# A scan's products one level behind and tied to projections, its states in two steps, and modulation passes in groups of four

## The chip, the cores and the metric

The kernel runs on one core of a Trainium2 chip. The metric is the device time of one execution in microseconds (us); of several executions the median is quoted. An execution profiled by the hardware shows each engine's instructions: TensorE (PE, with its weight loads as PEld), VectorE (DVE), ScalarE (ACT), GpSimd (POOL), and the DMA queue of SyncE (SP).

## What is computed

The reference is one inference step of a small diffusion backbone with two layers, width 1024, for 128 context tokens and 512 latent tokens, all in 32-bit floats. Layer 0 mixes its 640 tokens by neighbourhood attention and by bidirectional gated linear attention (four heads, key width 64, value width 128); layer 1 by grouped-query attention. Each layer ends in a ConvFFN, and each sublayer is modulated by vectors that come from the conditioning through a matrix of 1024 x 6144 a layer. The change concerns the linear attention:

```python
def step(s, inp):                       # one chunk of 64 tokens, one direction
    qc, kc, vc, gc = inp
    bcum = jnp.cumsum(gc.astype(jnp.float32), axis=2)
    o_inter = jnp.einsum('bhid,bhde->bhie', qc * jnp.exp(bcum).astype(qc.dtype), s)
    ...
    att = jnp.einsum('bhid,bhjd,bhijd->bhij', qc, kc, decay)
    o = o_inter + jnp.einsum('bhij,bhje->bhie', att, vc)
    k_dec = kc * jnp.exp(blast - bcum).astype(kc.dtype)
    s_new = exp(blast) * s + jnp.einsum('bhjd,bhje->bhde', k_dec, vc)
```

and the modulation, `jax.nn.silu(cvec) @ w + bias`.

## The kernel before

Every large matrix product is a projection of three matmuls per tile, since operands are split into a high and a low part. `step` (L149 to L153) makes tiles named mm with 320 columns, `tokens_major` (L592 to L594) makes tiles named tm with 256 columns. Their weights come as ws tiles by DMA (L127); ScalarE rounds them to wh (L111), and VectorE or GpSimd forms the rest wl (L112).

The linear attention works on two head pairs, 0 and 1, in pieces that `layer0` calls in the order of `ORDER = ("a0", "s0", "a1", "o0", "q0", "s1", "o1")`: a for `gla_scores`, s for `gla_states`, o for `gla_out`; q puts the neighbourhood's query and key projection at the head of the queue.

- `gla_scores` takes seven levels (the products of tile lev) and then two wide ones, 32 and 64 (tile off). A level is a chain over four engines: VectorE subtracts cumulated gates into ea (L852) and eb (L853), ScalarE takes exponentials (L832), GpSimd multiplies ea by keys (L858) and VectorE multiplies eb by queries (L859); then 40 small matmuls on TensorE (L872), which use both, a masked copy acc on VectorE (L877) and an addition on GpSimd (L879). The wide levels' matmuls (L894, L898) are copied by ScalarE into att (L903), and VectorE sets the levels' sums in (L907).
- `gla_states` makes, for each direction, decayed keys kd on ScalarE and GpSimd, four transposes kdt on TensorE (L933), a copy kt on ScalarE (L935), eight matmuls ds (L940) and, on VectorE, state updates S (L945, L946).
- `gla_out` makes decayed queries qd and the outputs go (L965 to L968).

Between the steps of these pieces the kernel hands out other work by `fill.some(n, m)`: n steps of a queue of projections and m modulation passes from a list aside. A pass is the DMA of a 128 x 512 tile wa (L313, three buffers) and two multiply-and-sum instructions on VectorE over it (L316, outputs junk and wa). 48 passes lie in this stage. `fill.some(0, 99)` before s0 hands out all that are left.

The code's order isn't the final one: a list scheduler sets each engine's stream, in which queue work given out by `fill.some` has priority. Each engine then executes its stream in order. Behind the scan stand the neighbourhood's loads on SP: values vw (L782), their context vc (L784) and the bias tiles (L1064), which the attention's scores nas add (L1075) before they are transposed (napt, L1083).

## Time and profile before

| | us |
|---|---|
| median of 3 runs (1725.24 to 1729.24) | 1727.22 |
| profiled execution | 1725.67 |
| its span, first to last instruction | 1723.9 |

The profiled execution has 1.77 us outside its span. Its mean granted TensorE clock is 0.975 of full speed. The profile is read in this order: the busy shares, the span cut into stretches, what TensorE waited for in the scan's stretch, and the timeline around those waits. A length in the timeline is that of one instruction or of a run of like ones; matmuls overlap, so their pitch is the difference of two starts.

### The profile page before, as it was taken

How to read it: one execution, taken by the hardware profiler on the slowest of the kernel's cores; microseconds unless marked ns; L12 is line 12 of the kernel's file. 1: busy time of each engine (PE TensorE's matmuls, PEld its weight loads, DVE VectorE, ACT ScalarE, POOL GpSimd, SP SyncE). 2: the span in 40 equal slices, each digit the busy share in tenths (PEclk: the TensorE clock that was granted, in tenths of full speed). 3: DMA queues.
4: the chain of work that ended last, by engine and by line, in shares of the span. 5: the costliest groups of instructions: out<-in, count | busy, mean ns of one | idle time of the engine just before them, and what ended most of it. 6: DMA issues, size and time to landing. Idle time of an engine off the chain costs nothing.

```text
span 1723.9 us, 33442 instructions
## 1 busy us (share of the span) xinstructions
PE 1633.0 (95%) x13142; PEld 1560.4 (91%) x13142; DVE 1255.2 (73%) x2767; ACT 741.9 (43%) x1681; POOL 205.5 (12%) x473
## 2 busy tenths in 40 slices
PE   7969698999999999999999999999999999999997
PEld 6868687879999999999998888888999999999997
DVE  5899944875899989996656987885776544663664
ACT  4443254453533323322335676775453322331342
POOL 2235441310200000000003310100100000000001
PEclk8999899999999999999998999999999999999999
DMA  8623323332254455454232200120222222222222
GB/s 318 210 88 134 102 81 106 91 93 98 84 167 160 147 164 185 153 151 132 70 120 82 76 21 14 43 63 24 76 74 75 73 74 74 75 76 83 73 68 69
DMA packets 68014, 175.22 MB, mean 102 GB/s; under 512 B 7920, under 2 KB 9744, under 8 KB 66832
## 3 DMA queue, kind: packets, MB, share of 16 engines
q1 hardware_dynamic: 67024, 171.48, 30.7%
q8 instruction: 103, 1.69, 0.4%
q0 software_dynamic: 832, 1.60, 0.3%
q14 instruction: 55, 0.45, 0.1%
HBM read 165.71 MB, written 7.34 MB: 100 GB/s over the span
## 4 chain that ended last, share of the span: by engine, by line
PE 78%; DVE 13%; DMA 3%; ACT 2%; issue 2%; SPq 1%; POOL 0%; ACTq 0%; DVEq 0%; POOLq 0%
PE mm L153 66%; PE gpo L1310 2%; DVE wa L316 2%; DVE junk L316 2%; PE gpt L1298 1%; DMA wa<-in_ada_wt_dram 1%; PE gs L1289 1%; DVE wl L112 1%; PE gs L1290 1%; DVE mx L1036 1%; PE napo L1102 1%; PE ss L410 1%; DVE eb L853 1%; DMA bias<-in_na_bias_dram 1%; DVE eb L859 1%
## 5 line engine op out<-in xcount | busy, mean ns | idle before, releaser
L153 PE MATMUL mm<-hh,wl 128*128 128x320 f32 x2080 | 651.0, 315 | 9.2 <-DVE wl L112 4.1
L153 PE MATMUL mm<-hl,wh 128*128 128x320 f32 x2080 | 647.7, 312 | 0.4 <-DVE hl L456 0.4
L153 PE MATMUL mm<-hh,wh 128*128 128x320 f32 x2080 | 641.3, 311 | 0.0
L111 ACT CAST wh<-ws 128x512 fp32r<-128x512 f32 x376 | 228.5, 614 | 435.3 <-PE mm L153 401.9
L153 PEld LDWEIGHTS mm<-hh,wl 128*128 128x128 f32 x2080 | 394.0, 190 | 19.2 <-issue 9.0
L153 PEld LDWEIGHTS mm<-hl,wh 128*128 128x128 f32 x2080 | 395.1, 190 | 2.7 <-DVE h L445 1.2
L153 PEld LDWEIGHTS mm<-hh,wh 128*128 128x128 f32 x2080 | 393.5, 190 | 0.6 <-issue 0.2
L112 DVE TENSOR_TENSOR wl<-ws,wh 128x512 fp32r<-128x512 f32 x348 | 239.1, 689 | 146.5 <-ACT wh L111 145.3
L153 PE MATMUL mm<-glo,wh 128*128 128x320 f32 x704 | 217.7, 310 | 0.0
L153 PE MATMUL mm<-ghi,wh 128*128 128x320 f32 x704 | 217.7, 310 | 0.0
L153 PE MATMUL mm<-ghi,wl 128*128 128x320 f32 x704 | 215.8, 310 | 0.0
L488 DVE SCALAR_TENSOR_TENSOR x<-mm,mod,x 128x192 f32<-128x192 f32 (+2 forms) x240 | 96.9, 435 | 88.9 <-PE mm L153 88.0
L153 PEld LDWEIGHTS mm<-ghi,wl 128*128 128x128 f32 x704 | 132.3, 189 | 1.3 <-issue 1.3
L153 PEld LDWEIGHTS mm<-glo,wh 128*128 128x128 f32 x704 | 133.0, 189 | 0.0
L153 PEld LDWEIGHTS mm<-ghi,wh 128*128 128x128 f32 x704 | 132.8, 189 | 0.1
L316 DVE SCALAR_TENSOR_TENSOR junk<-wa,sb 128x512 f32<-128x512 f32 x160 | 116.9, 734 | 6.7 <-DMA wa<-in_ada_wt_dram 6.4
L316 DVE SCALAR_TENSOR_TENSOR wa<-wa,sb 128x512 f32<-128x512 f32 x160 | 118.2, 745 | 0.3
L522 POOL MEMSET u<- 128x1 f32 x88 | 8.5, 98 | 761.1 <-DVE gate L515 426.6
L525 ACT COPY u<-mm 128x320 f32<-128x320 f32 x88 | 37.7, 431 | 87.8 <-PE mm L153 82.1
L592 PE MATMUL tm<-wl,hh 128*128 128x256 f32 x200 | 58.9, 300 | 7.4 <-ACT v L601 4.4
L1042 ACT ACTIVATE gp<-gs,mx,rq 128x640 f32<-128x640 f32 x64 | 57.0, 891 | 17.3 <-DVE mx L1038 11.6
L528 ACT COPY u<-mm 128x192 f32<-128x192 f32 x88 | 28.4, 323 | 79.8 <-PE mm L153 79.8
(302 smaller groups left out, 2432.5 us busy)
## 6 DMA issues: line engine op xcount, KB each, us to landing
ws<-in_wu_dram SPq DMA_DIRECT2D x88, 512.0 KB, 3.5
wa<-in_ada_wt_dram SPq DMA_DIRECT2D x160, 256.0 KB, 3.1
ws<-in_wd_dram SPq DMA_DIRECT2D x32, 448.0 KB, 3.8
aw<-in_ada_w_dram SPq DMA_DIRECT2D x8, 1024.0 KB, 14.2
ws<-in_w_ab_dram SPq DMA_DIRECT2D x16, 512.0 KB, 10.5
ws<-in_wd_dram SPq DMA_DIRECT2D x16, 512.0 KB, 3.6
x<-in_xT_dram SPq DMA_DIRECT2D x16, 320.0 KB, 4.5
ws<-in_w_gqa_dram SPq DMA_DIRECT2D x10, 512.0 KB, 3.5
```

The costliest lines, as they stand in the source:

```text
L111: nc.scalar.copy(hi, src)
L112: eng.tensor_tensor(lo, src, hi, ALU.subtract)
L153: nc.tensor.matmul(ps, x, y[:, s], start=st, stop=sp_)
L316: nc.vector.scalar_tensor_tensor(w if v else junk, w, 1.0, cs[v, j], ALU.mult, ALU.mult, accum_out=acc[:, k, v, j:j + 1])
L410: nc.tensor.matmul(ps[0:rows, c:c + 2], part[:, t], onesd, start=True, stop=True)
L488: nc.vector.scalar_tensor_tensor(x[:, b:e], ps[:, b - HN * h:e - HN * h], gate[:, v, m:m + 1], old[:, b:e], ALU.mult, ALU.add)
L525: nc.scalar.copy(u[:, 1:321], ps)
L528: nc.scalar.copy(u[:, 321:513], ps[:, 0:192])
L592: nc.tensor.matmul(ps, hh[:, s], wlo, start=(k == 0), stop=False)
L853: nc.vector.tensor_tensor(v(eb), sides(NT, h, 1), sides(g, f, 0), ALU.subtract)
L1042: nc.scalar.activation(dst, src, AF.Exp, bias=mx[:, i:i + 1], accum_out=sm[:, i:i + 1], **kw)
L1310: last = nc.tensor.matmul(po[64 * f:64 * f + 64, 0:128], vs[t][:, 64 * kv:64 * kv + 64], mates[f]["x"][:, 128 * t:128 * t + 128], start=(t ...
```

## The change

Four things are changed in the code. Products of a level (matmuls, masked copy, addition) are made after the next level's sides have been requested, with one more `fill.some(RLEV)` before level 64. Matmuls of products, transposes and states are tied behind the newest projection matmul that the queue has given out, so the scheduler can't put them ahead of it. `gla_states` makes both directions' transposes and copies first and then both directions' matmuls and updates. And passes come four at a time at each s and o piece, with the rest after the last piece.

```diff
@@ -146,11 +146,13 @@
 
         return part
 
+    newest = [None]
+
     def step(ps, w, k, hh, hl, h, start, stop):
         whi, wlo = w(k)
         s = slice(h * HN, h * HN + HN)
         for (x, y, st, sp_) in ((wlo, hh, start, False), (whi, hl, False, False), (whi, hh, False, stop)):
-            nc.tensor.matmul(ps, x, y[:, s], start=st, stop=sp_)
+            newest[0] = nc.tensor.matmul(ps, x, y[:, s], start=st, stop=sp_).ins
 
     def together(srcs, H, done, make=None, raws=None, n=1024):
 
@@ -240,7 +242,14 @@
 
 
         def __init__(self):
-            self.queue, self.aside, self.owed, self.after = [], [], 0.0, None
+            self.queue, self.aside, self.owed, self.after, self.newest = [], [], 0.0, None, None
+
+        def behind(self):
+
+            tie = ExitStack()
+            if self.newest is not None:
+                tie.enter_context(tc.issue_after(self.newest))
+            return tie
 
...
@@ -263,6 +272,7 @@
                     self.queue.pop(0)
                 else:
                     n -= 1
+                    self.newest = newest[0]
 
...
@@ -591,7 +601,7 @@
                     whi, wlo = ws[k // 4](k % 4)
                     nc.tensor.matmul(ps, hh[:, s], wlo, start=(k == 0), stop=False)
                     nc.tensor.matmul(ps, hl[:, s], whi, start=False, stop=False)
-                    nc.tensor.matmul(ps, hh[:, s], whi, start=False, stop=(k == KD - 1))
+                    newest[0] = nc.tensor.matmul(ps, hh[:, s], whi, start=False, stop=(k == KD - 1)).ins
...
@@ -757,15 +767,17 @@
                     att.update(gla_scores(m, kg[m], qg[m], cum[m], fill))
                 elif kind == "s":
                     fill.until(g_vg)
-                    fill.some(0, 99)
+                    fill.some(0, SST)
                     gla_states(m, kg[m], cum[m], vg, S, fill)
                 elif kind == "o":
+                    fill.some(0, SST)
                     last = gla_out(m, qg[m], cum[m], vg, att, S, OT, fill)
                 else:
                     fill.first(nxt)
 
             for p in ORDER:
                 piece(p[0], int(p[1]))
+            fill.some(0, 99)
...
@@ -861,15 +873,15 @@
 
         accs = C("acc")
         acc, tmp = accs[:, 0:320], accs[:, 320:640]
-        for li, h in enumerate(LEVELS):
-            A, B = (k, q) if h == 0 else level(h)
+        def products(li, A, B):
             ps = PS("lev")
...
+            with fill.behind():
+                for t in range(5):
...
@@ -877,27 +889,38 @@
             nc.vector.tensor_tensor(w.rearrange("p (e t i) -> p e t i", e=2, i=32), pv, mk, ALU.mult)
             if li:
                 nc.gpsimd.tensor_tensor(acc[:, 0:320], acc[:, 0:320], tmp[:, 0:320], ALU.add)
+
+
+        ready = None
+        for li, h in enumerate(LEVELS):
+            sides = (li, k, q) if h == 0 else (li, *level(h))
+            if ready:
+                products(*ready)
+            ready = sides
             fill.some(RLEV, SLEV)
         A32, B32 = level(32)
+        products(*ready)
+        fill.some(RLEV)
         A64, B64 = level(64)
         fill.some(ROFF, SOFF)
         big, small = PS("off"), PS("offx")
         res = {}
         blocks = [(e, slice(64 * e, 64 * e + 64), t, big[:, e, 128 * t:128 * t + 128] if t < 4 else small[:, e, 0:128])
                   for e in range(2) for t in range(5)]
-        for width in (32, 64):
...
+        with fill.behind():
+            for width in (32, 64):
...
@@ -926,19 +949,25 @@
             nc.gpsimd.tensor_tensor(x[:, 0:NT], x[:, 0:NT], k[:, 0:NT], ALU.mult)
             expo(de, end)
             kd[d], dec[d] = x, de
-        for d in range(2):
-            tiles = (0, 1, 2, 4) if d == 0 else (3, 2, 1, 4)
+        order = [(0, 1, 2, 4), (3, 2, 1, 4)]
+        kts = []
+        for d, tiles in enumerate(order):
             pt = P1("kdt")
-            for i, t in enumerate(tiles):
-                nc.tensor.transpose(pt[:, 128 * i:128 * i + 128], kd[d][:, 128 * t:128 * t + 128], ident)
+            with fill.behind():
+                for i, t in enumerate(tiles):
+                    nc.tensor.transpose(pt[:, 128 * i:128 * i + 128], kd[d][:, 128 * t:128 * t + 128], ident)
             kt = T("kt", "v2", n=512)
             nc.scalar.copy(kt[:, 0:512], pt)
-            ds = P1("ds")
-            for i, t in enumerate(tiles):
-                for e, pe in col_pairs():
-                    h = 2 * m + e
-                    nc.tensor.matmul(ds[pe, 128 * i:128 * i + 128], kt[:, 128 * i + 64 * e:128 * i + 64 * e + 64],
-                                     vg[t][:, 128 * h:128 * h + 128], start=True, stop=True)
+            kts.append(kt)
+            fill.some(RST / 2)
+        for d, tiles in enumerate(order):
+            kt, ds = kts[d], P1("ds")
+            with fill.behind():
+                for i, t in enumerate(tiles):
+                    for e, pe in col_pairs():
+                        h = 2 * m + e
+                        nc.tensor.matmul(ds[pe, 128 * i:128 * i + 128], kt[:, 128 * i + 64 * e:128 * i + 64 * e + 64],
+                                         vg[t][:, 128 * h:128 * h + 128], start=True, stop=True)
             s = C("S")[:, 0:NT].rearrange("p (t e) -> p t e", e=P)
             nc.sync.dma_start(s[:, 0, :], a["gla_s"][d, m])
             for i, t in enumerate(tiles[0:3]):
@@ -946
...
-            fill.some(RST)
+            fill.some(RST / 2)
@@ -1489,6 +1518,7 @@
 ROUT = 6
 SLEV = 2
 SOFF = 4
+SST = 4
```

Each engine has the same set of instructions as before; only their order differs (a line such as L316 is L326 in the changed code). On TensorE, at the states of pair 0, before:

```order
670 L933 MATMUL kdt<-ident,kd 128x128 x4
671 L872 MATMUL lev<-kqg 32x32 x18
...
690 L592 MATMUL tm<-wl,hh 128x256
691 L940 MATMUL ds<-v,kt 64x128 x8
692 L933 MATMUL kdt<-ident,kd 128x128 x4
693 L593 MATMUL tm<-wh,hl 128x256
...
717 L593 MATMUL tm<-wh,hl 128x256
718 L940 MATMUL ds<-v,kt 64x128 x8
719 L872 MATMUL lev<-eb,kqg 32x32 x40
```

and now (tm are filler projections, lev the first products of pair 1):

```order
666 L958 MATMUL kdt<-ident,kd 128x128 x4
...
690 L604 MATMUL tm<-wh,hh 128x256
691 L958 MATMUL kdt<-ident,kd 128x128 x4
...
701 L602 MATMUL tm<-wl,hh 128x256
702 L969 MATMUL ds<-v,kt 64x128 x8
703 L603 MATMUL tm<-wh,hl 128x256
...
706 L603 MATMUL tm<-wh,hl 128x256
707 L969 MATMUL ds<-v,kt 64x128 x8
708 L604 MATMUL tm<-wh,hh 128x256
```

Both transposes stand ahead of both state products, ten filler matmuls lie between, and the products of pair 1 stand behind them. On VectorE, in the scores of pair 1, with buffer numbers (wa and junk are the passes, eb_2354 and ea_2444 sides of levels), before:

```order
269 L877 TENSOR_TENSOR acc_2087<-lev_2188,mask32_112 128x320
270 L853 TENSOR_TENSOR eb_2354<-cum_789 128x640
271 L316 SCALAR_TENSOR_TENSOR junk_1954,adacc_1876<-wa_1952,sb_770 128x512
272 L316 SCALAR_TENSOR_TENSOR wa_1947,adacc_1876<-wa_1947,sb_773 128x512
273 L945 SCALAR_TENSOR_TENSOR S_2056<-S_2056,dec_1975,ds_2047 128x128
274 L599 COPY v_2141<-tm_2238 128x256
275 L852 TENSOR_TENSOR ea_2444<-cum_789 128x640
276 L853 TENSOR_TENSOR eb_2443<-cum_789 128x640
277 L316 SCALAR_TENSOR_TENSOR wa_1952,adacc_1876<-wa_1952,sb_776 128x512
278 L320 TENSOR_TENSOR mod04_1957<-adacc_1876 128x8
279 L859 TENSOR_TENSOR eb_2354<-eb_2354,kqg_739 128x640
280 L877 TENSOR_TENSOR acc_2087<-lev_2272,mask32_112 128x320
```

and now:

```order
262 L326 SCALAR_TENSOR_TENSOR wa_2807,adacc_2510<-wa_2807,sb_773 128x512
263 L974 SCALAR_TENSOR_TENSOR S_1943<-S_1943,dec_1859,ds_1934 128x128
264 L975 COPY S_1943<-ds_1934 128x128
265 L889 TENSOR_TENSOR acc_1995<-lev_2043,mask32_112 128x320
266 L864 TENSOR_TENSOR ea_2135<-cum_789 128x640
267 L865 TENSOR_TENSOR eb_2134<-cum_789 128x640
268 L864 TENSOR_TENSOR ea_2234<-cum_789 128x640
269 L871 TENSOR_TENSOR eb_2134<-eb_2134,kqg_739 128x640
270 L889 TENSOR_TENSOR acc_1995<-lev_2142,mask32_112 128x320
...
294 L871 TENSOR_TENSOR eb_2628<-eb_2628,kqg_739 128x640
295 L930 COPY att_2718<-acc_1995 32x5x32 x4
297 L326 SCALAR_TENSOR_TENSOR junk_2941,adacc_2510<-wa_2939,sb_770 128x512
```

The last rows of passes in pair 1's scores end with wa_2807; the last three passes stand behind the att copies (junk_2941 is the first), and the levels 2 to 64 between have none. On TensorE, at the end of pair 1's scores, before:

```order
865 L594 MATMUL tm<-wh,hh 128x256
866 L894 MATMUL off<-eb,ea 32x64
867 L592 MATMUL tm<-wl,hh 128x256
868 L894 MATMUL off<-eb,ea 32x64
...
921 L592 MATMUL tm<-wl,hh 128x256
922 L593 MATMUL tm<-wh,hl 128x256
923 L594 MATMUL tm<-wh,hh 128x256
924 L894 MATMUL off<-eb,ea 32x64 x5
...
928 L898 MATMUL off<-eb,ea 64x64 x8
...
932 L153 MATMUL mm<-hh,wl 128x320
```

and now:

```order
897 L602 MATMUL tm<-wl,hh 128x256
898 L603 MATMUL tm<-wh,hl 128x256
899 L604 MATMUL tm<-wh,hh 128x256
900 L917 MATMUL off<-eb,ea 32x64 x16
901 L917 MATMUL offx<-eb,ea 32x64 x4
...
904 L155 MATMUL mm<-hh,wl 128x320
905 L155 MATMUL mm<-hl,wh 128x320
906 L155 MATMUL mm<-hh,wh 128x320
...
914 L921 MATMUL off<-eb,ea 64x64 x8
915 L921 MATMUL offx<-eb,ea 64x64 x2
...
918 L155 MATMUL mm<-hl,wh 128x320
```

Single off matmuls no longer alternate with tm, and the 48 tm matmuls that stood between the first off matmuls and the rest are gone from there; ten mm stand between the 32-wide and the 64-wide products.

Two more differences in the order matter below. From pair 1's last product to the state matmuls of pair 1 there were 48 mm, and now there are 38; and those sixteen state matmuls now follow both kt copies, where eight followed one copy each. On SP, three of the eight vw issues now stand ahead of the ws issue that stood ahead of them all.

## Rows read from the trace of the kernel before

**Rows 1.** The page: busy time of the engines (time, share of the span, instructions), and the shares of the engines in the chain of work that ended last.

```profile
PE 1633.0 (95%) x13142; PEld 1560.4 (91%) x13142; DVE 1255.2 (73%) x2767; ACT 741.9 (43%) x1681; POOL 205.5 (12%) x473
...
PE 78%; DVE 13%; DMA 3%; ACT 2%; issue 2%; SPq 1%; POOL 0%; ACTq 0%; DVEq 0%; POOLq 0%
```

**Rows 2.** The span cut into stretches of 43 us; here the three that hold head pair 0's scores (from 86 us on) and head pair 1's. Columns: stretch, its length, busy time (instructions) of PE, PEld, DVE, ACT and POOL, mean granted TensorE clock as a share of full speed, DMA share, GB/s.

```profile
86.00:129.00 43.00, 30.25 (x437) 28.12 (x437) 42.79 (x75) 20.82 (x40) 13.73 (x7) 0.92 0.26 89
129.00:172.00 43.00, 38.76 (x638) 36.01 (x638) 42.55 (x80) 16.32 (x36) 21.45 (x14) 0.92 0.39 133
172.00:215.00 43.00, 27.84 (x581) 25.96 (x575) 42.08 (x79) 11.97 (x20) 18.85 (x14) 0.84 0.31 104
```

**Rows 3.** What TensorE waited for from 86 to 300 us, by line and releaser: total us, times, longest us. The five largest.

```profile
PE lev L872 <- DVE eb L859: 8.6, 4, 5.0
PE ds L940 <- ACT kt L935: 7.5, 2, 7.2
PE napt L1083 <- DVE nap L1050: 6.4, 1, 6.4
PE tm L592 <- ACT v L601: 4.4, 2, 2.7
PE mm L153 <- DVE wl L112: 4.1, 1, 4.1
```

**Rows 4.** The timeline, in order of time on each engine: start us, length us, engine, line, operation, tiles, and in brackets idle time before it and its releaser. First TensorE at the end of pair 0's scores (the first projection matmul after them, and two more of the same run, 15 matmuls apart); then ScalarE; then TensorE at the states of pair 0 and in the scores of pair 1.

```profile
160.14 0.41 PE L153 MATMUL mm<-hh,wl 128*128 128x320 f32 x1
...
160.54 0.31 PE L153 MATMUL mm<-hh,wh 128*128 128x320 f32 x1
...
162.74 0.31 PE L153 MATMUL mm<-hh,wh 128*128 128x320 f32 x1
...
180.96 0.74 ACT L832 ACTIVATE eb<-eb 128x640 f32<-128x640 f32 x1 [9.94 <-DVE eb L853]
...
183.69 1.97 PE L940 MATMUL ds<-v,kt 128*64 128x128 f32 x16 [7.18 <-ACT kt L935]
...
195.80 0.39 PE L592 MATMUL tm<-wl,hh 128*128 128x256 f32 x1 [2.33 <-DVE v L599]
...
214.03 1.08 PE L872 MATMUL lev<-eb,ea 64*32 64x32 f32 x80 [5.02 <-DVE eb L859]
```

**Rows 5.** The timeline at the end of pair 1's scores: VectorE's last modulation pass and its last product of these scores, and on TensorE two product matmuls (off) with one projection matmul between them, two projection matmuls 20 apart, and the first projection matmul behind all products.

```profile
197.14 0.68 DVE L316 SCALAR_TENSOR_TENSOR wa<-wa,sb 128x512 f32<-128x512 f32 x1
...
218.72 1.24 DVE L859 TENSOR_TENSOR eb<-eb,kqg 128x640 f32<-128x640 f32 x1 [0.53 <-ACT eb L832]
...
219.02 0.30 PE L894 MATMUL off<-eb,ea 64*32 64x64 f32 x2
219.56 0.30 PE L894 MATMUL off<-eb,ea 64*32 64x64 f32 x2
...
223.06 0.28 PE L592 MATMUL tm<-wl,hh 128*128 128x256 f32 x1
...
225.40 0.28 PE L594 MATMUL tm<-wh,hh 128*128 128x256 f32 x1
...
230.40 0.41 PE L153 MATMUL mm<-hh,wl 128*128 128x320 f32 x1
```

**Rows 6.** Groups of instructions: first VectorE's from 86 to 222 us (a pass is one junk and one wa row; L859 and L853 belong to a level of the scores), then the page's group of the pass's first half over the whole span. Columns: count, busy us, mean ns of one, idle before and releaser.

```profile
L316 DVE SCALAR_TENSOR_TENSOR wa<-wa,sb 128x512 f32<-128x512 f32 x33 | 29.8, 913 | 0.1
L316 DVE SCALAR_TENSOR_TENSOR junk<-wa,sb 128x512 f32<-128x512 f32 x32 | 28.5, 896 | 0.9 <-DMA wa<-in_ada_wt_dram 0.7
L859 DVE TENSOR_TENSOR eb<-eb,kqg 128x640 f32<-128x640 f32 x14 | 17.5, 1268 | 0.5 <-ACT eb L832 0.5
L853 DVE TENSOR_TENSOR eb<-cum 128x640 f32<-128x640 f32 x14 | 16.5, 1177 | 0.0
...
L316 DVE SCALAR_TENSOR_TENSOR junk<-wa,sb 128x512 f32<-128x512 f32 x160 | 116.9, 734 | 6.7 <-DMA wa<-in_ada_wt_dram 6.4
```

**Rows 7.** The timeline of one level of pair 1's scores behind the passes (level 64): VectorE's second difference, ScalarE's exponential of it, GpSimd's product of the other side. The product on VectorE that follows is in rows 5.

```profile
216.36 1.49 DVE L853 TENSOR_TENSOR eb<-cum 128x640 f32<-128x640 f32 x1
...
217.94 0.74 ACT L832 ACTIVATE eb<-eb 128x640 f32<-128x640 f32 x1 [0.67 <-DVE eb L853]
...
217.35 1.92 POOL L858 TENSOR_TENSOR ea<-ea,kqg 128x640 f32<-128x640 f32 x1 [0.18 <-ACT ea L832]
```

**Rows 8.** The timeline at the states of pair 1: the first copy of a transposed decayed key on ScalarE and the state matmuls that wait for it on TensorE; and one of VectorE's waits from 86 to 300 us.

```profile
247.68 0.59 ACT L935 COPY kt<-kdt 128x512 f32<-128x512 f32 x1
...
248.33 1.09 PE L940 MATMUL ds<-v,kt 128*64 128x128 f32 x16 [0.35 <-ACT kt L935]
...
DVE kcl L112 <- ACT qd L832: 7.9, 1, 7.9
```

**Rows 9.** SyncE's DMA queue (start us, time in which issues of that line ran, line, tile): weights, values of the neighbourhood, their bias; the longest wait in it; and what VectorE waited for at the bias.

```profile
249.17 0.33 SPq L127 DMA_DIRECT2D ws<-in_w_ab_dram  x1
249.55 5.52 SPq L782 DMA_DIRECT2D vw<-values  x5
...
269.74 12.99 SPq L1064 DMA_DIRECT2D bias<-in_na_bias_dram  x3
...
SPq L127 <- DVE wl L112: 24.8, 3, 12.9
...
DVE nas L1075 <- DMA bias<-in_na_bias_dram: 7.2, 1, 7.2
```

More of the change, by code (lines that the diff above doesn't have):

```diff
@@ L863, in gla_scores @@
         acc, tmp = accs[:, 0:320], accs[:, 320:640]
-        for li, h in enumerate(LEVELS):
-            A, B = (k, q) if h == 0 else level(h)
+        def products(li, A, B):
             ps = PS("lev")
-            for t in range(5):
-                for e in range(2):
-                    pe = slice(64 * e, 64 * e + 64)
-                    for j in range(4):
-                        s = slice(128 * t + 32 * j, 128 * t + 32 * j + 32)
-                        nc.tensor.matmul(ps[32 * j:32 * j + 32, e, 32 * t:32 * t + 32], A[pe, s], B[pe, s], start=True, stop=True)
+            with fill.behind():
+                for t in range(5):
+                    for e in range(2):
+                        pe = slice(64 * e, 64 * e + 64)
+                        for j in range(4):
+                            s = slice(128 * t + 32 * j, 128 * t + 32 * j + 32)
+                            nc.tensor.matmul(ps[32 * j:32 * j + 32, e, 32 * t:32 * t + 32], A[pe, s], B[pe, s], start=True, stop=True)
             pv = ps[:, :, 0:160].rearrange("p e (t i) -> p e t i", i=32)
@@ L887, in gla_scores @@
                   for e in range(2) for t in range(5)]
-        for width in (32, 64):
-            for e, pe, t, dst in blocks:
-                if width == 32:
-                    for j in range(4):
-                        b = j // 2
-                        s = slice(128 * t + 32 * j, 128 * t + 32 * j + 32)
-                        nc.tensor.matmul(dst[32 * j:32 * j + 32, 64 * b:64 * b + 64], A32[pe, s],
-                                         B32[pe, 128 * t + 64 * b:128 * t + 64 * b + 64], start=True, stop=True)
-                    continue
-                for b in range(2):
-                    nc.tensor.matmul(dst[64 * b:64 * b + 64, 64 - 64 * b:128 - 64 * b],
-                                     A64[pe, 128 * t + 64 * b:128 * t + 64 * b + 64],
-                                     B64[pe, 128 * t + 64 - 64 * b:128 * t + 128 - 64 * b], start=True, stop=True)
+        with fill.behind():
+            for width in (32, 64):
+                for e, pe, t, dst in blocks:
+                    if width == 32:
+                        for j in range(4):
+                            b = j // 2
+                            s = slice(128 * t + 32 * j, 128 * t + 32 * j + 32)
+                            nc.tensor.matmul(dst[32 * j:32 * j + 32, 64 * b:64 * b + 64], A32[pe, s],
+                                             B32[pe, 128 * t + 64 * b:128 * t + 64 * b + 64], start=True, stop=True)
+                        continue
+                    for b in range(2):
+                        nc.tensor.matmul(dst[64 * b:64 * b + 64, 64 - 64 * b:128 - 64 * b],
+                                         A64[pe, 128 * t + 64 * b:128 * t + 64 * b + 64],
+                                         B64[pe, 128 * t + 64 - 64 * b:128 * t + 128 - 64 * b], start=True, stop=True)
         for e in range(2):
```

## The prediction

> **What bounds the kernel now.** The page comes first. TensorE is busy for 95% of the span and holds 78% of the chain that ended last; VectorE holds 13% [rows 1]. So nearly everywhere the time is TensorE's, and a new order can win only where TensorE stands idle. The span in stretches says where that is. In the three stretches from 86 to 215 us VectorE is busy for 42.79, 42.55 and 42.08 of 43 us while TensorE has 30.25, 38.76 and 27.84, and in the last of them the granted clock falls to 0.84 [rows 2]. That is the linear attention's scan: passes and levels share VectorE, which is the bound here, and TensorE has projections for cover but stands behind small products that wait. The waits name them: 8.6 us for VectorE's product L859, 7.5 us for the copy kt, then 6.4 us at napt behind the scan, which the bias causes (below), 4.4 and 4.1 us for a value tile and a weight rest [rows 3]. In the order of time, four places follow pair 0's scores: ds waits 7.18 us at 183.69, a filler matmul 2.33 us at 195.80, lev 5.02 us at 214.03 [rows 4]; and the last products of pair 1 come late, though VectorE made their last side at 218.72 + 1.24 = 219.96: TensorE reaches the projection behind them at 230.40, since filler stood between [rows 5].
>
> The sum below is made against the profiled execution, 1725.67 us. The median of the three runs is 1.55 us above it, and that is added at the end.
>
> **Part 1, pair 0's scores (86 to 160.1 us).** The instructions are the same on every engine, and VectorE has under half a microsecond free in each of the two stretches [rows 2]. One level of lag takes waits from TensorE, but a bound engine has to do the same work before the last product. I take 0. The ends are 3 us either way: a lost 2 to 3 us is the size of one wait in the list (the longest for a value tile is 2.7), and as much could come back where VectorE meets GpSimd less.
>
> **Part 2, states of pair 0 and scores of pair 1 (160.1 to 230.4 us).** This is the change's main part. Before, the copy kt stood on ScalarE behind exponentials which waited 9.94 us for VectorE's differences, which waited behind passes [rows 4]. Now both transposes and copies come ahead of these exponentials, and ds has ten filler matmuls in front. That wait of 7.18 us goes. What is late next is the level itself: VectorE's stream up to pair 1's level 2 still holds 45 of the 48 passes, so TensorE will wait before level 2 instead. I therefore don't add up TensorE's waits; I time VectorE's last product.
> VectorE has only three passes fewer ahead of it. In this stretch the halves of a pass take 913 and 896 ns, against 734 for the first half over the whole span [rows 6], so three passes cost 3 x 1.81 = 5.4, or 3 x 2 x 0.734 = 4.4 us undisturbed. I take 5.0. Against that stands new idle time: with no passes between, the product L859 follows its own difference and must wait for the exponential. In level 64 the difference ended at 216.36 + 1.49 = 217.85, the exponential ran from 217.94 to 218.68, and the product began at 218.72, so an uncovered level leaves 0.87 us [rows 5, 7]. Five levels, of which the order covers about half with value copies and weight rests: 0 to 4.4 us, taken 2. So the last product ends at 219.96 - 5.0 + 2 = 217.0. Behind it TensorE has only the last products, which take about 1 us (a run of 80 small ones took 1.08 [rows 4]): 218.0. Before it was 230.4. **Gain 12.4 us.**
> The two ends. TensorE's own work is the lower one: from level 2's products it has 120 tm at (225.40 - 223.06) / 20 = 0.117 us [rows 5], four lev runs at 1.08 or less, ten mm at (162.74 - 160.54) / 15 = 0.147 [rows 4], and some 2 us of wide products: 14.0 + 4.3 + 1.5 + 2 = 21.8. Level 2 can't start before the passes in front are done, some 5 us before the 197.14 at which the last pass began [rows 5], thus near 192, and the end would be 213.8: gain 16.6. The other end is VectorE with all its new idle time and 3 us from part 1: 223.4, gain 7.
> Two smaller terms lie in here. Off matmuls that stood singly between tm cost 0.54 us for one step [rows 5], where one tm costs 0.117; now they come in one run. And ten mm more are done by this point than before, 10 x 0.147 = **1.5 us more**, by the count of the order.
> The first rule that I weigh is on the clock. Rows show 0.84 in the stretch with the two long waits and 0.92 in the two before [rows 2]; 0.84 is a mean of stretches at 2.4 and at 1.2 GHz. The Trainium skill ("TensorE: Matmul & The Clock Gate", HAM oscillation) says that a wait before every batch of matmuls throws the engine back to the low clock each time. By that rule the tied order, with its one wait per level, could keep the clock low through pair 1; it is the slower rival below. The trace agrees as far as the 0.84 goes.
>
> **Part 3, outputs, states of pair 1 (230 to 256 us).** With ten mm fewer in front, TensorE reaches the sixteen ds sooner than the copies are there. Before, the first ds began 248.33 - 230.40 = 17.9 us after the last product, 0.35 us late, with 48 mm in that stretch; ScalarE's copy began 17.3 us after it and took 0.59 [rows 5, 8]. Now TensorE needs 17.9 - 1.5 = 16.4, and less by the 0.6 us of waits, while two copies have to be made: 17.3 + 2 x 0.59 = 18.5. **Loss 2.5 us**, between 1 and 4. The three late passes with their sums stand on VectorE ahead of kcl and two weight rests. They take 4.4 to 5.4 us; VectorE waited there for 7.9 us in one piece before [rows 8], so they cost nothing. Without that cover a weight rest would be up to 5 us late and TensorE with it.
> The second rule speaks against passes at this place. GpSimd multiplies decayed queries and keys there, and a pass on VectorE reads two tiles; L859, which does too, shows a mean of 1268 ns in the scan's stretch [rows 6]. The Trainium skill ("GPSIMD Engine Reference", Key points) names contention with VectorE instructions that have two SBUF inputs. By it the three passes would take 5.4 and not 4.4 us, still inside the 7.9. The trace agrees with it in rows 6.
>
> **Part 4, the bias.** The scores wait 7.2 us for a bias tile, and TensorE 6.4 us at napt behind that [rows 3, 9]. On SP the eight vw issues began at 249.55, behind a ws that had waited 12.9 us for VectorE's wl, and the bias issues at 269.74 ran for 12.99 [rows 9]. Three of the vw now stand ahead of that ws. So this queue can move earlier at least as far as TensorE does, and the wait stays as it is: 0. If it moves further, up to 6.4 us are gained; if the ws wait hangs on a later event than now, as much is lost.
>
> **Behind 300 us** the order is that of before, and I take no term.
>
> **Sum.** 0 - 12.4 - 1.5 + 2.5 + 0 = -11.4; 1725.67 - 11.4 = 1714.3 in the profiled execution, **1715.8** for the median.
>
> **The rivals.**
> (a) Nothing much comes of it, since VectorE stays the bound. Rows 2 speak for it: VectorE has no free time until 215. Then all uncovered exponentials cost their 0.87 us, masked copies wait for TensorE, which now comes later to its products, and the last product ends where it ended; TensorE still saves the filler behind it, but loses part 3's 4 us and half of the rest to the bias: about 3 us, 1724. Against it: 48 tm stood behind VectorE's end before, and they are ahead of it now; 48 x 0.117 = 5.6 us of TensorE's work.
> (b) TensorE becomes the bound: 16.6 + 1.5 gained, no wait for kt (copies come early because ScalarE is idler), 5 of the bias's 6.4 us gained. 1727.2 - 23 = 1704.
> (c) Slower. One mechanism: TensorE, tied to filler, waits once per level and stays at 1.2 GHz through pair 1. At half the clock a tm takes twice its 0.117 us, 0.234 (an estimate). The 120 tm then take 28 us, lev, mm and wide products about 9, and the end is 192 + 37 = 229, a gain of 1.4 + 1.5; the copies cost 4, and the bias, whose queue waits for weight rests of this stretch, 6: 7.1 us slower, 1734. It decides once the waits per level exceed what a level's filler covers, that is if a level on VectorE takes over 36 x 0.117 + 1.08 = 5.3 us. Rows 6 and 7 give two differences, a product and 0.87: 2 x 1.18 + 1.27 + 0.87 = 4.5, with the masked copy about 5. That is close below, and so this rival stays.
> (d) The scheduler's order doesn't do what the words say. The passes show this: of 48 only three have moved behind pair 1. Part 2 has it in its sum already.
>
> **How the numbers follow.** The forecast's own case, with 1709 to 1721, 0.58; (b) 0.12; (a) 0.18; (c) 0.12. About 0.2%, 3.5 us, is what a measurement tells from no change. Faster by more than that: all of the forecast, (b) and a quarter of (a), 0.75; within: most of (a) and a little of (c), 0.15; slower: 0.10. The range leaves out the fast half of (b) and the slow part of (c): 1704 to 1727.
>
> **What would show it.** Right: the wait of ds for kt at pair 0 is gone; the first projection behind pair 1's products starts at 214 to 221 instead of 230.40; VectorE's last L859 ends near 217; a wait of 1 to 4 us for kt at pair 1; the clock from 172 to 215 above 0.84. Wrong: VectorE's last product at 220 or later, or a wait of TensorE in front of every lev; or a bias wait much above 6.4 us, which would eat a gain that the scan shows.

## The result and the profile after

The changed kernel takes 1717.29 us (median of 4 runs, 1716.58 to 1718.1); the kernel before took 1728.23 beside it (1725.24 to 1731.15). The ratio is 0.9929, 95% interval 0.9906 to 0.9953: 10.9 us faster. The profiled execution took 1717.48 us with a span of 1715.7, so the two profiled executions are 8.2 us apart; the one of before lies 2.6 us below its median, the one of after at its median. The bookkeeping below explains the 8.2.

First the stretches, as in rows 2 (same columns), of the changed kernel:

```profile
86.00:129.00 43.00, 37.10 (x418) 34.41 (x416) 42.78 (x82) 21.15 (x41) 11.58 (x6) 1.00 0.42 135
129.00:172.00 43.00, 30.45 (x562) 28.49 (x563) 41.42 (x69) 15.94 (x35) 23.39 (x14) 0.80 0.33 103
172.00:215.00 43.00, 40.20 (x743) 37.15 (x742) 37.43 (x69) 13.24 (x23) 21.82 (x15) 0.92 0.31 103
```

VectorE is no longer full from 172 to 215 us (37.43 of 43 us), and TensorE has 40.20 there instead of 27.84. What TensorE waited for from 86 to 300 us, the five largest, against rows 3:

```profile
PE tm L602 <- ACT v L611: 4.6, 2, 2.5
PE offx L917 <- DVE acc L889: 3.9, 1, 3.9
PE go L994 <- ACT got L1001: 3.6, 2, 2.2
PE lev L884 <- DVE mod L330: 3.3, 1, 3.3
PE lev L884 <- DVE eb L871: 3.1, 2, 1.6
```

The waits of ds for kt and of napt for the bias are gone. A new one is go for got: pair 1's outputs need the buffer that ScalarE empties by copying pair 0's outputs into got. The end of pair 1's scores in the timeline, as in rows 5, VectorE's last product and the first projection behind all products:

```profile
219.40 1.91 DVE L871 TENSOR_TENSOR eb<-eb,kqg 128x640 f32<-128x640 f32 x1
...
222.59 0.42 PE L155 MATMUL mm<-hl,wh 128*128 128x320 f32 x1
```

VectorE ends at 221.31, later than the 219.96 of before; TensorE is through 1.28 us after it, where it took 10.44 us [rows 5]. So the time came from filler that no longer stood behind the last products, and not from VectorE. What VectorE did up to that product reads in the stretch from the first gate matmul, where the scan starts, to its end, before and now, and in what it waited for there, before (first two waits) and now:

```profile
77.32:219.96 142.64, 110.48 (x1727) 101.46 (x1727) 139.33 (x258) 54.41 (x102) 57.34 (x36) 0.89 0.33 112
78.11:221.31 143.20, 120.87 (x1865) 111.42 (x1865) 135.51 (x243) 56.21 (x106) 62.39 (x38) 0.90 0.35 115
...
DVE junk L316 <- DMA wa<-in_ada_wt_dram: 1.7, 5, 0.4
DVE eb L859 <- ACT eb L832: 0.5, 1, 0.5
...
DVE junk L326 <- DMA wa<-in_ada_wt_dram: 3.8, 4, 1.6
DVE eb L871 <- ACT eb L844: 2.6, 3, 0.9
```

It works 3.8 us less (139.33 to 135.51) and stands idle 4.4 us more (3.3 to 7.7), for exponentials and for the loads of the passes.

Behind that, most of it is lost again. The same work, up to the first score nas of the neighbourhood, took 230.40 to 262.77 us before and takes 222.59 to 260.76 now: 38.17 us instead of 32.37, though ten mm fewer are left. The first score and, for what follows below, the first output of the context's attention (ctxo), before and now:

```profile
262.77 0.39 PE L1071 MATMUL nas<-kk,q 128*128 128x256 f32 x1
303.26 0.67 PE L1145 MATMUL ctxo<-ctxx,v 128*64 128x128 f32 x4 [0.46 <-ACT ctxx L1140]
...
260.76 0.36 PE L1100 MATMUL nas<-kk,q 128*128 128x256 f32 x1 [1.30 <-ACT kk L708]
296.19 0.44 PE L1174 MATMUL ctxo<-ctxx,v 128*64 128x128 f32 x4 [0.46 <-ACT ctxx L1169]
```

The timeline of ScalarE and TensorE shows where the time goes:

```profile
232.86 0.62 ACT L111 CAST kch<-kc 128x512 fp32r<-128x512 f32 x1 [3.75 <-DMA kc<-in_na_kc_dram]
235.58 0.62 ACT L111 CAST kch<-kc 128x512 fp32r<-128x512 f32 x1 [2.10 <-DMA kc<-in_na_kc_dram]
...
237.52 2.50 PE L994 MATMUL go<-att,v 128*128 128x128 f32 x10 [2.21 <-ACT got L1001]
242.10 2.50 PE L994 MATMUL go<-att,v 128*128 128x128 f32 x10 [1.35 <-ACT got L1001]
...
245.26 3.10 PE L969 MATMUL ds<-v,kt 128*64 128x128 f32 x32
```

and what SyncE's queue waited for from 215 to 300 us:

```profile
SPq L801 <- DVE junk L326: 4.5, 2, 2.8
```

SyncE's loads of the context keys kc wait 4.5 us for junk of the late passes. Both tiles come from one ring of three buffers, N. ScalarE waits for the keys with the copies got behind them, and TensorE for got. What that costs beyond the waits is in stretches of 10 us from 222 us on:

```profile
222.00:232.00 10.00, 10.00 (x98) 9.43 (x92) 7.92 (x13) 6.04 (x17) 6.98 (x4) 1.00 0.31 100
232.00:242.00 10.00, 6.53 (x43) 5.63 (x42) 5.50 (x15) 7.01 (x13) 3.49 (x2) 0.77 0.31 102
242.00:252.00 10.00, 9.90 (x68) 9.09 (x68) 6.07 (x12) 6.06 (x13) 3.31 (x4) 0.72 0.33 105
```

The granted clock, a mean of time at 2.4 and at 1.2 GHz, is 0.77 in the stretch in which TensorE is idle for a third, and 0.72 in the next. The sixteen state matmuls take 3.10 us there (the run from 245.26), where before each half took 1.09 [rows 8]; and the two runs of go of pair 1 take 2.50 us each, where before they took

```profile
243.54 1.28 PE L965 MATMUL go<-att,v 128*128 128x128 f32 x10
...
246.18 1.38 PE L965 MATMUL go<-att,v 128*128 128x128 f32 x10 [0.31 <-ACT got L972]
```

That is 3.3 us for the slower matmuls and 3.3 us more of waits for got (3.6 against 0.3), together most of the 5.8 and of the 1.5 us for ten mm.

Then comes the gain that lasts. From the first score to ctxo took 262.77 to 303.26 us, 40.5, and now 260.76 to 296.19, 35.4. The bias no longer comes late. SyncE's queue, against rows 9; then two of its waits before, that of the ws in front of the values and that of a bias issue for the bias before it, and the second of these now:

```profile
233.28 1.83 SPq L794 DMA_DIRECT2D vw<-values  x3
...
245.99 5.58 SPq L794 DMA_DIRECT2D vw<-values  x5
...
268.17 6.65 SPq L1093 DMA_DIRECT2D bias<-in_na_bias_dram  x3
...
SPq L127 <- DVE wl L112: 11.2, 1, 11.2
SPq L1064 <- DMA bias<-in_na_bias_dram: 10.6, 1, 10.6
...
SPq L1093 <- DMA bias<-in_na_bias_dram: 1.6, 1, 1.6
```

The bias issues begin hardly sooner (268.17 us, 269.74 before). What has changed is how soon the tile is there: 1.6 us of waiting instead of 10.6. Before, the last vw, vc and a ws were issued right ahead of it, until 269.65; now all vw are out by 251.57 and the last ws by 262.10. That the bias then stood behind their transfers fits this order; the transfers weren't followed one by one. The ws in front of the values had waited 11.2 us for a weight rest; the 12.9 of rows 9, which the prediction puts there, belong to a ws behind the bias.

### The profile page after: what moved, and what is told of

Same layout as the page of the kernel before. It is cut to its first block, busy times and chain, and to the rows that moved or that the text cites. A ratio compares the mean times of both kernels' runs of the same rounds, so it can differ in the third digit from the quotient of the medians.

```text
span 1715.7 us, 33434 instructions
## 1 busy us (share of the span) xinstructions
PE 1635.8 (95%) x13142; PEld 1563.1 (91%) x13142; DVE 1258.2 (73%) x2767; ACT 742.4 (43%) x1681; POOL 208.9 (12%) x473
## 4 chain that ended last, share of the span: by engine, by line
PE 79%; DVE 13%; ACT 3%; DMA 2%; issue 2%; POOL 1%; SPq 0%; ACTq 0%; DVEq 0%; POOLq 0%
PE mm L155 66%; DVE junk L326 2%; PE gpo L1339 2%; DVE wa L326 2%; PE gpt L1327 1%; DVE wl L112 1%; DMA wa<-in_ada_wt_dram 1%; PE gs L1318 1%; PE gs L1319 1%; DVE mx L1065 1%; PE ss L420 1%; PE tm L602 1%; PE napo L1131 1%; PE tm L604 1%; PE tm L603 1%
## 5 line engine op out<-in xcount | busy, mean ns | idle before, releaser
L112 DVE TENSOR_TENSOR wl<-ws,wh 128x512 fp32r<-128x512 f32 x348 | 243.5, 702 | 150.5 <-ACT wh L111 149.3
L326 DVE SCALAR_TENSOR_TENSOR junk<-wa,sb 128x512 f32<-128x512 f32 x160 | 120.8, 760 | 7.2 <-DMA wa<-in_ada_wt_dram 6.9
L326 DVE SCALAR_TENSOR_TENSOR wa<-wa,sb 128x512 f32<-128x512 f32 x160 | 114.3, 721 | 0.3
```

The lines of the kernel that those rows point to most:

```text
L112: eng.tensor_tensor(lo, src, hi, ALU.subtract)
L326: nc.vector.scalar_tensor_tensor(w if v else junk, w, 1.0, cs[v, j], ALU.mult, ALU.mult, accum_out=acc[:, k, v, j:j + 1])
```

## Experiments

One table for all, so that each run can be read by stage. It has, in us, the start of the last off matmul of pair 1's scores counted from the first gate matmul (the start of the stage moves by 1 to 3 us between kernels, so it is taken out), then the stretches from there to the first nas, to the first ctxo and to the last nas, all from views of the tiles on TensorE; each column holds the same work, but that the kernels with lag have ten mm more done at the first mark (1.5 us). The ratios are of medians, the stretches of one profiled execution each, which lies up to 3 us from its median (lag_only 2.4 above, bias_before 2.9 above, st_only and st_old 2.5 below), so small differences in a column may be the execution's.

| kernel | ratio to before (95%) | scan | to first nas | to ctxo | to last nas |
|---|---|---|---|---|---|
| before | 1 | 152.8 | 32.7 | 40.5 | 77.9 |
| changed | 0.9929 (0.9906 to 0.9953) | 144.2 | 38.5 | 35.4 | 76.7 |
| p_early | 0.9940 (0.9927 to 0.9953) | 146.7 | 35.8 | 35.9 | 79.1 |
| p_last | 1.0015 (1.0004 to 1.0026) | 139.3 | 52.0 | 36.2 | 78.2 |
| no_tie | 0.9942 (0.9928 to 0.9955) | 142.0 | 38.7 | 35.9 | 77.8 |
| st_old | 0.9960 (0.9948 to 0.9972) | 145.3 | 38.7 | 38.1 | 78.9 |
| no_lag | 0.9997 (0.9983 to 1.0010) | 151.4 | 42.7 | 35.1 | 79.1 |
| lag_only | 0.9987 (0.9974 to 1.0001) | 149.3 | 41.2 | 37.9 | 78.0 |
| st_only | 0.9977 (0.9967 to 0.9988) | 152.8 | 32.7 | 33.9 | 79.9 |
| p_only | 1.0006 (0.9998 to 1.0015) | 150.3 | 38.8 | 40.1 | 77.4 |
| lag_st | 0.9936 (0.9920 to 0.9952) | 150.5 | 33.9 | 34.3 | 76.5 |
| bias_before | 0.9943 (0.9925 to 0.9962) | 154.2 | 32.6 | 34.9 | 78.0 |
| bias_after | 0.9992 (0.9983 to 1.0001) | 151.6 | 38.7 | 36.1 | 79.6 |
| junk_tied | 1.0166 (1.0143 to 1.0188) | 149.2 | 34.9 | 36.0 | 79.3 |

**Passes.** In the changed kernel, all of them early:

```diff
                     fill.until(g_vg)
-                    fill.some(0, SST)
+                    fill.some(0, 99)
                     gla_states(m, kg[m], cum[m], vg, S, fill)
                 elif kind == "o":
-                    fill.some(0, SST)
...
-            fill.some(0, 99)
```

> The changed kernel, but all passes that are left are handed out at the states of pair 0, as before; no pass stands behind pair 1's scores. Theory of the prediction (VectorE bounds pair 1's scores, a pass ahead of its end costs its length): VectorE's last product some 5 us later than the 221.4 us of the changed kernel, 1720 to 1722 us. Rival read from the changed kernel's trace (the three late passes hold the buffer that the neighbourhood's context keys need, ScalarE waits 3.75 + 2.10 us for those keys ahead of the copies of pair 1's outputs, and TensorE 2.21 + 1.35 us for these): these waits go, and the time is 1715 to 1718 us.

It gave 1719.95 us. Both theories were half right (the got in the way are pair 0's): VectorE's last product ended at 224.50 instead of 221.31, and the way to the first nas got 2.7 us shorter, with one wait of 1.7 us for got left. The two cancel within the intervals. The low clock stayed (0.66 from 242 to 252 us), so the late passes aren't all that makes this way longer than before.

The other way, with passes behind pair 1's scores:

```diff
-                    fill.some(0, SST)
+                    fill.some(0, SST if m == 0 else 0)
                     gla_states(m, kg[m], cum[m], vg, S, fill)
                 elif kind == "o":
-                    fill.some(0, SST)
...
-            fill.some(0, 99)
...
             kcl.append(y.rearrange("p (h t) -> p h t", h=4))
+        fill.some(0, 99)
```

> The changed kernel, but the passes of the last s and of both o pieces are handed out only after the context keys are loaded, so seven passes stand behind pair 1's scores and none of them holds the keys' buffer. If VectorE bounds pair 1's scores and the late keys cost TensorE about 4 us: VectorE's end 5 to 7 us earlier, TensorE's own work becomes the bound (about 214 us), 1708 to 1712 us. If VectorE isn't what sets the end of pair 1's scores: only the keys' part, 1713 to 1715 us. If passes behind the scores delay states and neighbourhood: 1717 us or more.

1731.38 us: in the total only the third held (1717 or more), and in the scan the first. Eleven passes stand behind pair 1's scores, not seven. These scores ended soonest of all kernels, counted from the stage's start, with TensorE busy for all of 172 to 215 us. Then it stood still. What TensorE and ScalarE waited for from 215 to 300 us:

```profile
PE gss L1012 <- ACT gsq L1009: 12.6, 1, 12.6
...
ACT gsq L1009 <- DVE junk L326: 12.9, 1, 12.9
```

The squares gsq of the scan's output are the next tiles of the same ring N. This is the keys' mechanism once more, and it shows the sign: a pass that moves off VectorE's path holds a buffer in the next stage.

Before with the passes of the change alone:

> The kernel before with one part of the change: passes four at a time, so that three stand behind pair 1's scores (no lag, no ties, states as before). If three passes ahead of VectorE's last product cost their length: the last products some 5 us earlier; the late passes then delay the context keys, so 1723 to 1727 us in all. If TensorE's filler behind the last products sets the end: 1727 to 1730 us.

1730.54 us, at the upper end of the second theory. VectorE's last product ended at 216.38, 3.6 us sooner and 3.0 counted from the stage's start:

```profile
76.71:216.38 139.67, 114.42 (x1724) 104.15 (x1724) 132.18 (x241) 54.22 (x102) 58.96 (x36) 0.88 0.34 113
```

VectorE works 7.2 us less than before in this stretch, but waits 4.2 us more (7.5 against 3.3), so of the three passes 1.0 us each is left. TensorE came to its mm at the end of the products only 10.9 us after that, as before, and the way to the first nas took 38.8 us, 6.1 more.

**Ties.** `behind` returns no tie (`if self.newest is not None:` becomes `if False:`).

> The changed kernel without the ties behind the newest projection matmul. If the ties bring the gain at pair 1's end (filler no longer behind the last products, waits of small products covered): most of the gain goes, 1723 to 1727 us. If lag, states and passes bring it: 1716 to 1719 us.

1719.26 us, and the scan is 2 us shorter without them. The ties aren't what took the filler away from behind the last products; no effect of them is shown.

**Lag.** `products(*sides)` straight after each level's sides, without the added `fill.some(RLEV)`, all else as changed:

> The changed kernel without the lag: a level's products come straight behind its sides, still tied, states and passes as changed. If the lag is what brings the gain at pair 1: 1724 to 1728 us. If passes and states do: 1717 to 1720 us. If tied products without lag wait for their sides with nothing behind them: above 1728 us.

1729.96 us, above what the first theory gives: nothing is left of the gain. TensorE was through 8.5 us after VectorE's last product (222.01) again. The lag it is that removes the filler there: with it the gap is 1.3 us in every kernel, without it 6.7 to 10.9. With the lag goes the added queue step ahead of level 64; the two weren't tried apart. It isn't free, as the lag alone shows:

> The kernel before with one part of the change: a level's products one level behind, with the added queue step (no ties, states and passes as before). The runs so far show that the ties aren't needed (1719.26 us without them, pair 1's last products done at 219.6). If the lag brings the end of pair 1's scores forward by itself: the last products end near 222 to 226 instead of 230.4, 1720 to 1724 us. If passes or states bring it: 1727 to 1729 us.

1728.4 us, the second theory's time (1721.74 to 1731.74; only no_lag spreads wider, 1721.35 to 1732.75). The gap closes, but VectorE's last product ends at 228.26, 8.3 us later than before and 5.6 counted from the stage's start. VectorE's stretch and its longest wait there, the passes' loads:

```profile
80.01:228.26 148.25, 125.14 (x1866) 113.54 (x1865) 138.91 (x258) 55.93 (x107) 60.90 (x38) 0.90 0.34 110
...
DVE junk L326 <- DMA wa<-in_ada_wt_dram: 6.4, 8, 1.6
```

It works as long as before and is idle 9.3 us instead of 3.3; the loads have 6.4 of these, 1.7 before. Why they come later isn't shown. Two smaller waits read in VectorE's timeline at two levels of pair 1, here of lag_st (below), which has the lag too:

```profile
207.67 1.23 DVE L869 TENSOR_TENSOR eb<-eb,kqg 128x640 f32<-128x640 f32 x1 [0.86 <-ACT eb L842]
211.68 0.49 DVE L887 TENSOR_TENSOR acc<-lev,mask 128x320 f32<-128x320 f32 x1 [2.77 <-PE lev L882]
...
215.19 1.24 DVE L869 TENSOR_TENSOR eb<-eb,kqg 128x640 f32<-128x640 f32 x1 [0.87 <-ACT eb L842]
```

A level's product stands right behind its own difference and waits 0.87 us for the exponential, and the masked copy waits for TensorE. Those are the terms of the prediction's rival (a); the loads aren't among them.

**States.** The old order of the two directions, in the changed kernel (transposes, kt, ds and updates of one direction, `fill.some(RST)`, then the other):

> The changed kernel with the states in the old order (transposes, copy and matmuls of one direction, then of the other), still tied. If the copy's wait of 7.18 us at pair 0 was worth its length: it returns in part and the time is 1720 to 1724 us. If VectorE bounds that stretch: 1716 to 1719 us, and at pair 1 the wait of the sixteen state matmuls goes, so it could be 1 us faster.

1722.93 us, as the first theory had it, but not for its reason: the scan is no longer (145.3 against 144.2), and no wait for kt at pair 0 came back. It lost on the way to ctxo. There VectorE waits again:

```profile
DVE nas L1100 <- DMA bias<-in_na_bias_dram: 4.2, 1, 4.2
```

The new order of states alone in the kernel before:

> The kernel before with one part of the change: both directions' transposes and copies ahead of both directions' state matmuls (no lag, no ties, passes as before). If the wait of 7.18 us for the copy was on the path: 1721 to 1724 us. If VectorE bounds that stretch and only takes the wait elsewhere: 1726 to 1729 us.

1724.36 us. The scan keeps its 152.8 us (a lev now waits where ds waited), the first nas comes as before, and the way to ctxo is 6.6 us shorter, of which 2.0 are lost again by the last nas:

```profile
PE lev L882 <- DVE eb L869: 15.7, 4, 9.2
```

The order on SP tells the two kinds apart. In before, p_only, st_old and lag_only, with the old states, a ws stands between the states' loads and all vw (37.9 to 40.5 us to ctxo); in changed, p_early, no_tie, st_only and lag_st three or four vw stand ahead of it (33.9 to 35.9). That ws waits for a weight rest (11.2 us in before).

Lag and states together, nothing else:

> The kernel before with two parts of the change: the lag and the states in two steps (no ties, passes as before). Alone the lag gave a ratio of 0.9987 and the states 0.9977; all four parts 0.9929. If the two need each other (the lag takes pair 1's last products forward, the states keep the neighbourhood's queue from giving it back): 1717 to 1721 us, about all of the gain. If their gains merely add: 0.9964, 1722 to 1723 us. If ties or passes are what makes the lag work: 1726 us or more.

1718.74 us: these two give all of the gain that can be told. They don't add; alone they gave 0.9987 and 0.9977. The lag's scan is hardly better (150.5), the way to ctxo is, and of the 6 to 10 us that p_only, lag_only and no_lag lose on the way to the first nas only 1.2 are left: no late pass holds the ring, and the granted clock is 1.00 from 252 to 282 us, where it is 0.84, 0.67 and 0.70 in lag_only. What in the states' new order keeps it up wasn't tried apart.

**The bias alone.**

```diff
-                nc.sync.dma_start(bias, a["na_bias"][h][:, bp:bp + 2, :])
+                nc.gpsimd.dma_start(bias, a["na_bias"][h][:, bp:bp + 2, :])
```

> The kernel before, with the neighbourhood's bias tiles issued on GpSimd's DMA queue and not behind weights and values on SyncE's. If the 6.4 us at napt were the bias's place in that queue and on the path: the wait goes, 1720 to 1723 us. If the weights behind take the time instead, or GpSimd's issues delay its other work: 1726 to 1730 us.

1720.44 us. With the issue on another queue and nothing else of the change, the way to ctxo is 34.9 us instead of 40.5, and most of the gain is there. VectorE's wait for the bias was 7.2 us [rows 9] and is now:

```profile
DVE nas L1075 <- DMA bias<-in_na_bias_dram: 1.3, 1, 1.3
```

The bias was on the path. The scheduler's order differs here too, from 53 us on, and the scan is 1.4 us longer.

> The changed kernel with the same move of the bias issues. If the change had already taken the bias wait away (no wait at napt is left in its trace, where 6.4 us were): 1716 to 1718 us, as the changed kernel. If the queue still held something back: below 1714 us. If GpSimd's issues cost: above 1719 us.

1727.7 us, which only the third theory allows (above 1719). The way to ctxo is as in the changed kernel (36.1 against 35.4), so the bias's part was indeed spent. But the scheduler, which saw other issues on GpSimd's queue, put the scan in another order (151.6 us instead of 144.2). Why that order is so much worse wasn't followed up.

**The ring.**

```diff
-                    junk = N("junk")[:, 0:512]
+                    junk = sp.tile([P, 512], mybir.dt.bfloat16, tag="adarow", name="junk")
...
                 elif kind == "o":
-                    fill.some(0, SST)
+                    with tc.issue_after(att["last"]) if m else ExitStack():
+                        fill.some(0, SST)
...
```

> The changed kernel, but the throwaway output of a pass's first half is a tile of its own (512 values in bfloat16, in the place of a small tile of the first modulation), not a buffer of the ring that the context keys and the output's squares use; and the passes of the last o piece are tied behind the last att copy, so that three passes still stand behind pair 1's scores. The stretch from pair 1's last product to the first score of the neighbourhood took 32.7 us before and 38.5 in the changed kernel, 33.9 with the lag and the states alone. If the ring is what the late passes cost: that stretch takes 33 to 35 us, pair 1's last product stays near 222, and the time is 1712 to 1715 us, below the changed kernel. If the late passes cost by their work on VectorE or their loads: 38 us there, and 1716 to 1719 us.

In its stage the ring's theory held: 34.9 us to the first nas instead of 38.5, with three passes still behind pair 1, and one wait of 1.7 us for got. The scan got longer, though (149.2), and the total is 1757.35 us, lost in later stages. Passes of the next stages come sooner (18 from 400 to 450 us, where the changed kernel has none) and stand among other work on VectorE, and from 376 to 1005 us TensorE waits for it:

```profile
PE rstd L441 <- DVE diag L383: 11.1, 2, 8.4
PE rstd L441 <- DVE mod L331: 7.3, 1, 7.3
```

In the changed kernel the first of these is 3.6 us from 372 to 966. So the ring that costs in one place seems to pace passes in others; the tie of the late passes, the other edit here, wasn't tried apart from it.

## Why the prediction came true, point by point

The total was right, 10.9 us measured for 11.4 forecast, but its terms were not: Part 2's gain was taken too large, Part 3's loss much too small, and Part 4, left at zero, gave 5.1 us. Of its own signs, the wait of ds is gone and the clock from 172 to 215 us is above 0.84; but the first projection behind pair 1's products starts at 222.59 (214 to 221 forecast), no wait for kt came at pair 1, and VectorE's last product "at 220 or later" was named as a sign of being wrong.

- **Part 1**, 0 forecast: pair 0's products end 5 us later (165.2 against 160.2), with 18 mm more done (2.6 us) and a stage that started 0.8 us later. A loss of about 1.5, inside its 3.
- **Part 2**, 12.4 + 1.5 forecast, 7.8 + 1.5 measured (230.40 to 222.59; Part 1's loss lies in it). The mechanism stood: the filler is gone from behind the last products, and a wait for kt isn't there. What failed is the sentence that VectorE's last product ends at 217.0. It ended at 221.31. In the sum's own terms, VectorE's work fell by 3.8 us where 5.0 was taken, and its idle time grew by 4.4 where 2 was taken: 2.1 for exponentials, as forecast, and 2.1 for the passes' loads, which the sum doesn't have (the lag alone brings 4.7 more of these). With the stage's start, 0.8 later, that is 4.4, the miss of 4.3. Passes alone (p_only) did give the 3.0 forecast for them (5.0 less 2); the sum has no cost of the lag on VectorE. Filler moved away was the whole gain, 10.44 - 1.28 = 9.2, less the 1.35 by which VectorE ends later.
- **Part 3**, a loss of 2.5 with bounds 1 and 4: 5.8 us more and 1.5 less left to do, 7.3. The failed step is "they cost nothing". It looked for cover on VectorE, and that was there; the passes held a ring's buffer, which a row of VectorE's idle time doesn't show. Without that hold the way is 2.7 us (p_early) and 3.6 us (junk_tied) shorter, so up to half of the 7.3 is the ring's; what brings the rest, with a wait of 1.7 us for got and a low clock in both, isn't shown. The two kt copies, which the term was made of, were no wait at all.
- **Part 4**, 0 between +6.4 and -6.4: 5.1 gained. The argument that SP can move earlier was right, and more came of it than the same wait at an earlier time, close to its upper bound. The ws wait that it names is 11.2 us, not 12.9. The runs show this as the part that lasts (st_only, bias_before).
- **Behind**, 0 forecast: 1.1 us (303.26 - 296.19 = 7.1 at ctxo, 8.2 at the end).

The sum: -7.8 - 1.5 + 7.3 - 5.1 - 1.1 = -8.2, the difference of the profiled executions. That this came close to -11.4 is luck: errors of opposite sign.

Of the rivals, (a) had part of its mechanism: uncovered exponentials and masked copies do set VectorE's end later, if less than the passes' loads, and the lag alone gave nothing clear of the noise. It lost since filler was moved by more than VectorE lost, and since the bias came on time. (b)'s bound, TensorE busy throughout, was reached only in p_last. A low clock as in (c) came, not in pair 1's levels but behind them, at 0.77 and 0.72. On the rule of "TensorE: Matmul & The Clock Gate" (HAM oscillation) in the Trainium skill, that a wait before each batch throws the clock back: from 172 to 215 us, in pair 1's levels, the trace shows little of it (0.92, and 0.84 before [rows 2]); from 129 to 172 it could (0.80, and 0.92 before), and behind pair 1 the clock is low after a wait. (d) was right as far as it went: what places passes is the scheduler and the ring, much more than the number given out.

Open: why lag_only and no_lag spread over 10 and 11 us between runs, why the passes' loads come later with the lag, why lag and states together give more than their sum, why GpSimd's queue changes the order so (bias_after), and what the ties do, of which no run shows an effect beyond the noise.

## What to carry to other kernels

When work is moved behind a stage, look up which buffer ring its throwaway outputs use: here the engine had room, and the next stage's loads and squares waited for the ring. A gain at a stage's end can be lost in the next one, and the wait behind that, here for a bias in an in-order queue, can be worth as much; undo each part by itself and compare by stages, since the total hid a gain of 9 us, a loss of 7 and another gain of 5. And a stage that looks bound by one engine can give time at its end alone, by what the waiting engine has queued behind the last product.

## What was not expected of the hardware

Three instructions of the late passes took 1.76, 2.04 and 2.02 us while GpSimd multiplied beside them, and the next 0.68, when it had stopped (at 231.71):

```profile
226.57 1.76 DVE L326 SCALAR_TENSOR_TENSOR junk<-wa,sb 128x512 f32<-128x512 f32 x1
...
228.27 2.04 DVE L326 SCALAR_TENSOR_TENSOR junk<-wa,sb 128x512 f32<-128x512 f32 x1
...
230.23 2.02 DVE L326 SCALAR_TENSOR_TENSOR wa<-wa,sb 128x512 f32<-128x512 f32 x1
...
232.19 0.68 DVE L326 SCALAR_TENSOR_TENSOR junk<-wa,sb 128x512 f32<-128x512 f32 x1
...
224.73 3.05 POOL L985 TENSOR_TENSOR qd<-qd,kqg 128x640 f32<-128x640 f32 x2 [3.58 <-ACT qd L844]
227.75 3.96 POOL L949 TENSOR_TENSOR kd<-kd,kqg 128x640 f32<-128x640 f32 x2
```

The contention that the Trainium skill names ("GPSIMD Engine Reference", Key points) is thus a factor of up to 3 for one instruction here, more than the 913 ns of the mean in rows 6 let one expect.
